# Mixing-stage weight loads issued by ACT behind its casts, and each S5 chunk's preparation on DVE in seven pieces: a layer of S5 and retention heads on one core

## The chip, the cores and the metric

The program runs on 1 core of a Trainium2 chip. The metric is the device time of one execution in microseconds (us); the time of a kernel is the median of its runs. TensorE (PE) multiplies matrices, VectorE (DVE), ScalarE (ACT) and GpSimd (POOL) work elementwise, SyncE (SP) issues DMAs; an engine that issues a DMA does it in the order of its own instructions, and waits there for what the DMA waits for. Each engine runs its instructions in order.

## The reference

One inference step of a layer, with 256 prompt tokens and 8 x 8 sampled tokens, which stand side by side as 320 columns. All arithmetic is fp32.

```python
h = rms_norm(x, norm_mix)
proj = h @ w_in                                  # 2048 x 5120
u, q, k, v, g = split(proj)                      # 5 x 1024 columns
s5_out = s5_mixer(u, ...)                        # 64 groups of 16 channels, 64 complex states each:
                                                 # bu = B u; x_t = lam x_(t-1) + bu_t; y = Re(C x) + d u
                                                 # gelu(y), then y * sigmoid(y @ w_glu + b)
qh, kh = rotary(q), rotary(k) / sqrt(128)        # 8 heads of 128
o, r = retention_chunked(qh, kh, vh, r0)         # (q k^T * decay mask) v + decayed q r0
ret = silu(g) * group_norm(o) * ret_gn_w
x = x + concat(s5_out, ret) @ w_out
gate, up = split(rms_norm(x, norm_ffn) @ w_ffn_in)
x = x + (silu(gate) * up) @ w_ffn_out            # width 5632
return rms_norm(x, norm_final), S5 states, retention states
```

## The kernel before, in words

Every weight matrix is cut into 128 x 128 blocks and read once. `wload` fetches up to eight blocks (128 x 1024 fp32, 512 KB) into a tile `raw`, ACT rounds it to the TensorE format (`hi`, the cast of L131), and DVE takes the rest (`lo = raw - hi`, L133). `gemm` then runs three matmuls for each block, hi by x's hi part, hi by x's lo part, lo by x's hi part (L143 to L145), with all 320 columns. `raw`, `hi` and `lo` have three buffers each, so that load n can start once the tiles of load n-3 are read. One input projection of 128 output columns takes two such loads. The loads are numbered here in the order of the program, from 0; loads 0 to 8 are those of the first four projections, which run together (L976 to L992), and 9 to 96 are the rest of the mixing stage.

The mixing stage (the first 400 us or so) goes through the heads h = 0 to 7: `do_q`, `do_k`, `do_v` (each a projection), for h < 4 also the gate `do_g`, for h < 6 also `do_u`, the S5 input of chunk h + 2; the gates of heads 4 to 7 follow, and then `w_out` for the retention half (`ps_o`). `rot` turns q and k (two copies `sw` on ACT, L748 and L749, three or four products and sums on DVE, among them `k_`). `head_k` transposes k (`pst`), multiplies q by k (`pss`) and scales the transposed k (`kd` on ACT, L765); `head_v` transposes v, ACT copies it (`vT`, L791, and `vs`, L792), and PE sums up the head (`po`, `psr`). DVE takes the statistics of `po` (BN_STATS, L822), POOL makes the scale of them (`gy`, L826 to L833), ACT normalizes (`on`, L839), and PE transposes the result (`pn`).

`s5_chunk(c)` handles an eighth of the S5 channels. It sends u through DRAM into another layout (`up_`, `via`, `kst`), prepares its coefficients on DVE (products `m` of `raw_bc` with the power tables `gpc` and `lpc`, sums `bl` and `cl`, the table `tb` from `e`, and `bst` from `btr` and `gtr`), then PE projects (`pb`) and makes the kernel `pk_`, which ACT copies (`toe`, L684), DVE scans, PE projects back (`py`), ACT and DVE add it up (`ev`), and SP sends it through DRAM again (`back`, `yc`). Then `y1 = d u + yc` on DVE and the GELU of it (ACT L727, L728, L730). In front of all this, the powers of the S5 eigenvalues are computed in many small operations on DVE (`scrt`, `ecs`, `lp`, `ff`, `gp`), copied by ACT into the tables (`lpc` L489, `gpc` L492, `gs` L501), and PE transposes `gs` (`pt`, L107), from which the rows `gtr` come.

PE's and POOL's order is the order in which the program writes them down. The chunks and heads are generators that yield a delay; after each weight block the program's own clock goes up by 0.4, and a generator whose delay has run out writes its next part there, between two blocks. The delays stand in the table `DL`. The order on DVE, ACT and SP is made by a scheduler from priorities (`high_priority`, `issue_after`) and its own costs.

Of the kernel before, what the change touches and what calls it, by code (L numbers as in the profile page):

```python
# [12 lines left out]
F32 = mybir.dt.float32  # L13
# [4 lines left out]
ADD, SUB, MUL = ALU.add, ALU.subtract, ALU.mult  # L18
PSUM = bass.MemoryType.PSUM

P = 128
# [11 lines left out]
CH = 4  # L33
NCP = NP // CH
# [10 lines left out]
def hybrid_kernel(ctx, tc, xT, w_in, w_in4, w_out, w_glu, w_fi, w_fo, vecs, s5p, bc, bt, x0,  # L45
# [3 lines left out]
    pe, act, dve, pool, sp = nc.tensor, nc.scalar, nc.vector, nc.gpsimd, nc.sync  # L49
# [68 lines left out]

    wpool = [wp, (3, 3, 3)]
    last_hi, last_raw, last_lo = [None], [None], [None]  # L120

    def wload(src, nk, offset=3000):

        out = []
        with tc.high_priority(offset=offset):
            for k0 in range(0, nk, 8):
                m = min(8, nk - k0)
                raw, hi, lo = (wpool[0].tile([P, 8, P], d, name=n, tag=n, bufs=wpool[1][i])
                               for i, (n, d) in enumerate((("raw", F32), ("hi", F32R), ("lo", F32R))))
                last_raw[0] = sp.dma_start(raw[:, :m], src[:, k0:k0 + m])  # L130
                cast = act.copy(hi[:, :m], raw[:, :m])  # L131
                last_hi[0] = cast
                last_lo[0] = dve.tensor_tensor(lo[:, :m], raw[:, :m], f(hi[:, :m]), SUB)  # L133
                out += [(hi[:, i], lo[:, i]) for i in range(m)]
        return out
# [41 lines left out]
    def tt(out, a, b, op):  # L177
        dve.tensor_tensor(out, a, b, op)
        return out
# [133 lines left out]
    lpc = s5.tile([P, 8, 2, 8, CH], F32, name="lpc")  # L313
# [248 lines left out]
        pool.tensor_tensor(ta, c8, s1, MUL)  # L562
        pool.tensor_tensor(tabl[:, 1], tabl[:, 1], ta, ADD)

    def s5_table(c):
# [5 lines left out]
        tb = s5.tile([P, 2, 4, NCP], F32, name="tb", tag="tb", bufs=1)  # L571
# [4 lines left out]
        tt(m2[:, 1], c8, s1, MUL)  # L576
        for r, op in enumerate((SUB, ADD)):
            tt(tb[:, r], m1[:, r].rearrange("p j a b -> p j (a b)"), m2[:, r].rearrange("p j a b -> p j (a b)"), op)
        return tb
# [43 lines left out]
    def s5_chunk(c):  # L623
# [16 lines left out]
                        raw[64 * g:64 * g + 64, 1, 4 * q:4 * q + 4], 1.0 - 2.0 * q)  # L640
        with tc.issue_after(rot_t["values"].ins):
            act.copy(d0[:, :, :, 1:], r4[:, js].unsqueeze(1).unsqueeze(3).to_broadcast([P, 2, 4, NCP - 1]))
        for w_, pc in ((0, gpc), (1, lpc)):
            dm = 3 - w_
            shm = [P, 8, CH, 16] if w_ else [P, 8, 16, CH]
            m1, m2 = (s5.tile(shm, F32, name=f"m{q}", tag=f"m{q}", bufs=1) for q in range(2))
            b_ = raw[:, w_].unsqueeze(dm).to_broadcast(shm)
            tt(m1, b_, pc[:, c, 0].unsqueeze(5 - dm).to_broadcast(shm), MUL)
            tt(m2, b_, pc[:, c, 1].unsqueeze(5 - dm).to_broadcast(shm), MUL)
            if w_ == 0:  # L650

                bl = s5.tile([P, 2, 2, 2, 16, CH], F32, name="bl", tag="bl", bufs=1)
                for r, (a, b, op) in enumerate(((m1[:, 0:4], m2[:, 4:8], SUB), (m1[:, 4:8], m2[:, 0:4], ADD))):
                    a, b = (t_.rearrange("p (u q) h s -> p u q (h s)", q=2) for t_ in (a, b))
                    tt(bl[:, r].rearrange("p q u h s -> p u q (h s)"), a, b, op)
                continue
            tt(cl[:, 0], m1[:, 0:4], m2[:, 4:8], SUB)
            tt(cl[:, 1], m1[:, 4:8], m2[:, 0:4], SUB)
        if c:
            tbl = s5_table(c)  # L660
        yield DL["b1"] + (4.0 if c == 0 else 0.0)
        if not c:
            tbl = s5_table(c)
        bst = s5_bst(c).rearrange("p q r s -> p r q s")
        load_bc(c + 2)
        yield DL["b2"]
        pb = ps_b.tile([P, 2, 512], F32, name="pb", tag="pb", bufs=1)
        for i in range(4):
            for u in range(2):
# [273 lines left out]
    def do_g(h):  # L943
        ps = proj(11 + 4 * h)
        sg = mp.tile([P, N], F32, name="sg", tag="sg", bufs=2)
        with tc.high_priority(offset=EVAC):
# [193 lines left out]
    rpool.close()  # L1140
    zhi = glp.tile([P, 8, N], F32R, name="zhi")
    zlo = glp.tile([P, 8, N], F32R, name="zlo")
    for n in range(8):
        ps = gemm("ps_g", w_glu[n], 8, yhi, ylo)
        with tc.issue_after(last_raw[0].ins):
            for g in range(2):
                sp.dma_start(vd[g::2, :, n].rearrange("h t e -> t h e"), vs[64 * g + NS * n:64 * g + NS * n + NS])
        sg = glp.tile([P, N], F32, name="sgl", tag="sgl", bufs=2)
        act.activation(sg, ps, AF.Sigmoid, bias=v("bglu", n))
        stt(sg, u32[:, n], 0.5, sg, MUL, MUL)  # L1150
        act.copy(zhi[:, n], sg)
        tt(zlo[:, n], sg, f(zhi[:, n]), SUB)
# [241 lines left out]
```

## Time and profile before

| | |
|---|---|
| median of 3 runs | 1443.73 us (1443.13 to 1445.22) |
| profiled execution | 1444.08 us, of which the span is 1442.3 us |
| mean granted TensorE clock | 0.994 |
| busy share of the span | PE 98%, DVE 68%, ACT 41%, POOL 8% |
| casts hi (L131) | 416, 969 ns each |
| differences lo (L133) | 416, 1125 ns each |
| weight loads of the mixing stage from `w_in` (L130) | 79 of 512 KB, each holding its issuer 0.33 us |

The span is one execution on the chip; the busy time of an engine holds no waiting. The views used are the waits (which engine waited at which line for which instruction of another, in us in total, times and the longest), the windows (busy time and number of instructions of each engine in a stretch, with the granted clock in the column after POOL, and the share and rate of the DMA engines), the timeline (start, duration, engine, line, operation, tiles, and the idle time before it with what ended it) and the chain of waits that ended last. Pieces overlap a little in the timeline, because an engine starts an instruction before the one before it has drained.

### The profile page before, as it was taken

To read this page: it belongs to the slowest core of one execution; us is meant where nothing else is said; L and a number is where in the kernel's file an instruction comes from. 1 tells how busy PE (TensorE), PEld (TensorE's weight loads), DVE (VectorE), ACT (ScalarE), POOL (GpSimd) and SP (SyncE) were. 2 spreads that over 40 slices of the span, in tenths; PEclk is the share of its full clock that TensorE was granted. 3 is DMA by queue.
4 is the path that set the end of the run, shared out by engine and by line. 5 is a ranking of instruction groups with operands and counts; after the bars stand their busy time and mean duration, and the time that the engine had idled before them with its cause. 6 is when DMAs were issued, how large, how long until landed. Compare 5 with 4: busy or idle time off the path is not lost.

```text
span 1442.3 us, 26157 instructions
## 1 busy us (share of the span) xinstructions
PE 1420.2 (98%) x10364; PEld 1407.3 (98%) x10364; DVE 973.8 (68%) x1917; ACT 591.8 (41%) x937; POOL 111.2 (8%) x177
## 2 busy tenths in 40 slices
PE   9999999999999999999999999999999999999996
PEld 9999999989999999999999999999999999999996
DVE  7988777788766746676777545767644677644554
ACT  7644545454355533333333333333333333333442
POOL 7620010011000000100000000000000000000001
PEclk9999999999999999999999999999999999999998
DMA  8565565555654466666757346666545765444442
GB/s 284 185 196 174 161 192 168 187 151 160 202 164 149 148 217 215 225 227 224 240 201 252 122 154 231 232 219 233 170 147 181 253 229 183 159 127 155 147 150 104
DMA packets 106363, 271.20 MB, mean 188 GB/s; under 512 B 30720, under 2 KB 44288, under 8 KB 106240
## 3 DMA queue, kind: packets, MB, share of 16 engines
q1 hardware_dynamic: 106096, 269.26, 56.2%
q8 instruction: 81, 1.33, 0.4%
q14 instruction: 42, 0.34, 0.1%
q10 hardware_dynamic: 144, 0.26, 0.1%
HBM read 258.44 MB, written 10.65 MB: 187 GB/s over the span
## 4 chain that ended last, share of the span: by engine, by line
PE 92%; DVE 3%; DMA 2%; ACT 2%; issue 0%; SPq 0%; DVEq 0%; ACTq 0%
PE ps_fo L143 7%; PE ps_fu L143 7%; PE ps_fu L144 7%; PE ps_fo L144 7%; PE ps_fo L145 7%; PE ps_fu L145 7%; PE ps_fg L143 7%; PE ps_fg L144 7%; PE ps_fg L145 7%; PE ps_p L143 5%; PE ps_p L145 5%; PE ps_p L144 5%; PE ps_o L143 2%; PE ps_o L144 2%; PE ps_o L145 2%; DVE lo L133 1%
## 5 line engine op out<-in xcount | busy, mean ns | idle before, releaser
L131 ACT CAST hi<-raw 128x1024 fp32r<-128x1024 f32 (+1 forms) x416 | 402.1, 969 | 674.9 <-PE ps_fo L144 187.9
L133 DVE TENSOR_TENSOR lo<-raw,hi 128x1024 fp32r<-128x1024 f32 (+1 forms) x416 | 467.4, 1125 | 299.1 <-ACT hi L131 296.7
L144 PE MATMUL ps_fo<-alo,hi 128*128 128x320 f32 x704 | 217.5, 309 | 0.0
L143 PE MATMUL ps_fg<-hhi,hi 128*128 128x320 f32 x704 | 217.5, 309 | 0.0
L143 PE MATMUL ps_fo<-ahi,hi 128*128 128x320 f32 x704 | 217.5, 309 | 0.0
L145 PE MATMUL ps_fo<-ahi,lo 128*128 128x320 f32 x704 | 217.5, 309 | 0.0
L144 PE MATMUL ps_fu<-hlo,hi 128*128 128x320 f32 x704 | 217.4, 309 | 0.0
L144 PE MATMUL ps_fg<-hlo,hi 128*128 128x320 f32 x704 | 217.4, 309 | 0.0
L145 PE MATMUL ps_fg<-hhi,lo 128*128 128x320 f32 x704 | 217.4, 309 | 0.0
L143 PE MATMUL ps_fu<-hhi,hi 128*128 128x320 f32 x704 | 217.4, 309 | 0.0
L145 PE MATMUL ps_fu<-hhi,lo 128*128 128x320 f32 x704 | 217.4, 309 | 0.0
L143 PE MATMUL ps_p<-xhi,hi 128*128 128x320 f32 x560 | 178.3, 318 | 1.6 <-ACT hi L131 1.6
L145 PE MATMUL ps_p<-xhi,lo 128*128 128x320 f32 x560 | 174.2, 311 | 0.7 <-DVE lo L133 0.7
L144 PE MATMUL ps_p<-xlo,hi 128*128 128x320 f32 x560 | 173.8, 310 | 0.0
L144 PEld LDWEIGHTS ps_fg<-hlo,hi 128*128 128x128 f32 x704 | 132.4, 188 | 0.0
L143 PEld LDWEIGHTS ps_fo<-ahi,hi 128*128 128x128 f32 x704 | 132.4, 188 | 0.0
L143 PEld LDWEIGHTS ps_fu<-hhi,hi 128*128 128x128 f32 x704 | 132.4, 188 | 0.0
L144 PEld LDWEIGHTS ps_fu<-hlo,hi 128*128 128x128 f32 x704 | 132.4, 188 | 0.0
L145 PEld LDWEIGHTS ps_fo<-ahi,lo 128*128 128x128 f32 x704 | 132.4, 188 | 0.0
L143 PEld LDWEIGHTS ps_fg<-hhi,hi 128*128 128x128 f32 x704 | 132.4, 188 | 0.0
L145 PEld LDWEIGHTS ps_fu<-hhi,lo 128*128 128x128 f32 x704 | 132.4, 188 | 0.0
L145 PEld LDWEIGHTS ps_fg<-hhi,lo 128*128 128x128 f32 x704 | 132.3, 188 | 0.0
(459 smaller groups left out, 2065.0 us busy)
## 6 DMA issues: line engine op xcount, KB each, us to landing
raw<-w_fi SPq DMA_DIRECT2D x176, 512.0 KB
raw<-w_in SPq DMA_DIRECT2D x79, 512.0 KB
raw<-w_fo SPq DMA_DIRECT2D x64, 512.0 KB
raw<-w_out SPq DMA_DIRECT2D x32, 512.0 KB
hi<-vd SPq DMA_DIRECT2D x32, 512.0 KB
lo<-vd SPq DMA_DIRECT2D x32, 512.0 KB
raw<-w_fo SPq DMA_DIRECT2D x64, 192.0 KB
rt<-r SPq DMA_DIRECT2D x8, 512.0 KB
```

Of the source, the lines that this page charges most:

```text
L131: cast = act.copy(hi[:, :m], raw[:, :m])
L133: last_lo[0] = dve.tensor_tensor(lo[:, :m], raw[:, :m], f(hi[:, :m]), SUB)
L143: pe.matmul(ps, hi, xhi[:, k], start=k == 0, stop=False)
L144: pe.matmul(ps, hi, xlo[:, k], start=False, stop=False)
L145: pe.matmul(ps, lo, xhi[:, k], start=False, stop=k == nk - 1)
```

## The change

`wload` no longer issues all raw loads on SP. While `on_act` is true, that is for loads 9 to 96, load n is issued by ACT, directly behind cast n-2. From the gated projection (`w_glu`) on, all loads stand on SP as before. So 88 loads move from SP's queue into ACT's.

In `s5_chunk` the preparation on DVE, which was written in two lumps around the yields `b1` and `b2`, is now written in seven pieces, each behind the last `lo` on DVE, with eight equal yields of the same sum (20.8, or 24.8 for chunk 0). The table function is cut in two for this. The delay `rows` goes from 11.0 to 12.5.

```diff
@@ wload
-                last_raw[0] = sp.dma_start(raw[:, :m], src[:, k0:k0 + m])
+                if on_act[0]:
+                    with tc.issue_after(casts[-2].ins) if len(casts) > 1 else ExitStack():
+                        act.dma_start(raw[:, :m], src[:, k0:k0 + m])
+                else:
+                    last_raw[0] = sp.dma_start(raw[:, :m], src[:, k0:k0 + m])
                 cast = act.copy(hi[:, :m], raw[:, :m])
+                casts.append(cast)
@@ s5_chunk
-        for w_, pc in ((0, gpc), (1, lpc)):
...
-        if c:
-            tbl = s5_table(c)
-        yield DL["b1"] + (4.0 if c == 0 else 0.0)
-        if not c:
-            tbl = s5_table(c)
-        bst = s5_bst(c).rearrange("p q r s -> p r q s")
-        load_bc(c + 2)
-        yield DL["b2"]
+        def paced(*fs):
+            with tc.issue_after(last_lo[0].ins):
+                return [g() for g in fs][-1]
+
+        step = (DL["b1"] + DL["b2"] + (4.0 if c == 0 else 0.0)) / 8
+        paced(lambda: powers(0, 0))
+        yield step
+        bl = paced(lambda: powers(0, 1), bl_sums)
+        yield step
+        paced(lambda: powers(1, 0))
+        yield step
+        paced(lambda: powers(1, 1), cl_sums)
+        yield step
+        em = paced(lambda: s5_table1(c))
+        yield step
+        tbl = paced(lambda: s5_table2(em))
+        yield step
+        bst = paced(lambda: s5_bst(c)).rearrange("p q r s -> p r q s")
+        yield step
+        load_bc(c + 2)
+        yield step
@@
-    DL = dict(b1=14.2, b2=6.6, scan=17.8, y=10.0, rows=11.0, k=8.5, v=6.1,
+    DL = dict(b1=14.2, b2=6.6, scan=17.8, y=10.0, rows=12.5, k=8.5, v=6.1,
@@ before the loop over w_glu
+    on_act[0] = False
```

(`powers(w_, q)` is one of the four products `m`, `bl_sums` and `cl_sums` the sums made of two of them.) A yield lets the program go on until its clock has passed the delay, and the clock moves in steps of a block, so PE's order moves with the yields: `pb` and `pk_` of a chunk stand 9 to 24 matmuls later among the matmuls of the projections, `py` 6 to 24 later, the two transposes `pt` 12 later. The scheduler, which has other dependences now, puts DVE and ACT into another order in many places. The changed file's lines are some 6 to 30 higher.

DVE around the turned k of head 0 (`k__737`; `lo` are the differences of the weights, `qg`, `qsp`, `ksp` parts of the turned q and k, `sg` a gate, `scrt`, `ecs`, `lp` the powers). Before:

```order
L178 TENSOR_TENSOR k__737<-ps_p,csr 128x320
L178 TENSOR_TENSOR sw<-sw,csr 128x320
L178 TENSOR_TENSOR ecs<-scrt 128x2x32
L178 TENSOR_TENSOR k__737<-k__737,sw 128x256
L178 TENSOR_TENSOR ksp<-k__737,sw 128x64
L178 TENSOR_TENSOR sg<-ps_p,rbc 128x320
L178 TENSOR_TENSOR lp<-rr,ecs 128x32 x2
L178 TENSOR_TENSOR scrt<-prm 128x32 x2
L178 TENSOR_TENSOR qg_111<-qsp,gqt 128x4x8
L133 TENSOR_TENSOR lo<-raw,hi 128x1024
```

And now:

```order
L184 TENSOR_TENSOR qsp<-q__727,sw 128x64
L184 TENSOR_TENSOR scrt<-prm 128x32
L184 TENSOR_TENSOR qg_111<-qsp,gqt 128x4x8 x2
L184 TENSOR_TENSOR scrt<-scrt 128x32
L442 RECIPROCAL scrt<-scrt 128x32
L184 TENSOR_TENSOR k__737<-ps_p,csr 128x320
L184 TENSOR_TENSOR sw<-sw,csr 128x320
L184 TENSOR_TENSOR sg<-ps_p,rbc 128x320
L139 TENSOR_TENSOR lo<-raw,hi 128x1024
L184 TENSOR_TENSOR k__737<-k__737,sw 128x256
L184 TENSOR_TENSOR ksp<-k__737,sw 128x64
L184 TENSOR_TENSOR sm<-pss,mk 128x256
```

The last sum of k, on which PE's transposes `pst` wait, has moved behind a gate, a difference lo and all the small operations that came after it, and stands directly ahead of `sm`, which needs PE's product of q and k.

ACT around the copies `gs` of the S5 powers, whose last four PE's transposes `pt` wait for. The casts here are those of loads 17, 18 and 19. Before:

```order
L131 CAST hi<-raw 128x1024
L492 COPY gpc<-gp 128x8x8 x6
L501 COPY gs<-gp 128x2x16 x6
L131 CAST hi<-raw 128x1024
L839 ACTIVATE on<-po,gy 128x128 x2
L508 COPY gt<-pt 128x256
L131 CAST hi<-raw 128x1024
```

And now:

```order
L136 CAST hi<-raw 128x1024
L133 DMA raw<-w_in 128x1024
L498 COPY gpc<-gp 128x8x8 x6
L136 CAST hi<-raw 128x1024
L133 DMA raw<-w_in 128x1024
L869 ACTIVATE on<-po,gy 128x128 x2
L507 COPY gs<-gp 128x2x16 x2
L136 CAST hi<-raw 128x1024
L133 DMA raw<-w_in 128x1024
L778 COPY sw<-ps_p 64x320
L779 COPY sw<-ps_p 64x320
L507 COPY gs<-gp 128x2x16 x4
```

Of the six copies four have moved behind two more casts, three loads and two copies `sw`. The last cast is that of load 19, and load 19 is the first DMA of this piece.

ACT around the head whose `po` stood at 319 us, head 7 (`v_r` is a cast of a finished head, `y` the GELU of an S5 chunk). Before:

```order
L727 ACTIVATE y_4333<-y_4332 128x320
L628 COPY up__4602<-u_118 128x320
L728 ACTIVATE y_4333<-y_4333,ones 128x320
L791 ACTIVATE vT<-pst_4361,rtok 128x128 x3
L1094 CAST v_r<-retp 128x320
L730 ACTIVATE y_4333<-y_4333 128x320
L131 CAST hi<-raw 128x1024
L792 COPY vs<-vT 64x128
```

And now:

```order
L638 COPY up__4609<-u_118 128x320
L821 ACTIVATE vT<-pst_4353,rtok 128x128 x3
L1124 CAST v_r<-retp 128x320
L136 CAST hi<-raw 128x1024
L133 DMA raw<-w_in 128x1024
L822 COPY vs<-vT 64x128
L757 ACTIVATE y_4363<-y_4362 128x320
```

The copies `vT` and `vs` of the head, for which PE's `po` waits, stood behind the first and second step of the GELU and now stand ahead of it; `vs` has a cast and a load ahead of it.

Two more places are told in words. In head 3 DVE had the statistics of `po` (L822) behind the two sums `tb` and three of the products `e` of a chunk's table, and now has these behind the statistics. And in five of the eight chunks `y1`, which waits for `yc`, has moved up on DVE ahead of a q, a k or a difference lo; in chunk 4 (`y1` at 282 us before) it now stands ahead of the lo of load 67 and of the turned k of head 6, and on ACT the GELU's first step, which waits for `y1`, stands ahead of cast 68 and its load, of `up_`, of cast 69 and its load and of `v_`, and `toe` behind all of these.

More of the change, by code (lines that the diff above doesn't have):

```diff
@@ L120, in hybrid_kernel @@
     last_hi, last_raw, last_lo = [None], [None], [None]
+    casts, on_act = [], [True]
     def wload(src, nk, offset=3000):
@@ L563, in s5_turns, with s5_table1 @@
         pool.tensor_tensor(tabl[:, 1], tabl[:, 1], ta, ADD)
-    def s5_table(c):
+    def s5_table1(c):
         js = slice(4 * c, 4 * c + 4)
@@ L570, in s5_table @@
         c8, s8 = (e18[:, 1, r, js].unsqueeze(3).to_broadcast(sht) for r in range(2))
-        tb = s5.tile([P, 2, 4, NCP], F32, name="tb", tag="tb", bufs=1)
         m1, m2 = (s5.tile([P, 2, 4, 8, 8], F32, name=f"e{q}", tag=f"m{q}", bufs=1) for q in range(2))
@@ L576, in s5_table, with s5_table2 @@
         tt(m2[:, 1], c8, s1, MUL)
+        return m1, m2
+    def s5_table2(ms):
+        m1, m2 = ms
+        tb = s5.tile([P, 2, 4, NCP], F32, name="tb", tag="tb", bufs=1)
         for r, op in enumerate((SUB, ADD)):
@@ L642, in s5_chunk, with powers @@
             act.copy(d0[:, :, :, 1:], r4[:, js].unsqueeze(1).unsqueeze(3).to_broadcast([P, 2, 4, NCP - 1]))
-        for w_, pc in ((0, gpc), (1, lpc)):
+        prods = {}
+        def powers(w_, q):
             dm = 3 - w_
+            pc = (gpc, lpc)[w_]
             shm = [P, 8, CH, 16] if w_ else [P, 8, 16, CH]
[L646 to L656, printed above, removed]
+            prods[q] = s5.tile(shm, F32, name=f"m{q}", tag=f"m{q}", bufs=1)
+            tt(prods[q], raw[:, w_].unsqueeze(dm).to_broadcast(shm),
+               pc[:, c, q].unsqueeze(5 - dm).to_broadcast(shm), MUL)
@@ new lines, in bl_sums, with cl_sums @@
+        def bl_sums():
+            m1, m2 = prods[0], prods[1]
+            bl = s5.tile([P, 2, 2, 2, 16, CH], F32, name="bl", tag="bl", bufs=1)
+            for r, (a, b, op) in enumerate(((m1[:, 0:4], m2[:, 4:8], SUB), (m1[:, 4:8], m2[:, 0:4], ADD))):
+                a, b = (t_.rearrange("p (u q) h s -> p u q (h s)", q=2) for t_ in (a, b))
+                tt(bl[:, r].rearrange("p q u h s -> p u q (h s)"), a, b, op)
+            return bl
+        def cl_sums():
+            m1, m2 = prods[0], prods[1]
```

## The prediction

> **What bounds the kernel now.** I read the busy times first, then PE's waits, then the windows around them, then each wait's cause in the timelines.
>
> ```profile
> PE 1420.2 (98%) x10364; PEld 1407.3 (98%) x10364; DVE 973.8 (68%) x1917; ACT 591.8 (41%) x937; POOL 111.2 (8%) x177
> ```
>
> PE does almost nothing but work. Neither SP's issue time nor the 41% of ACT decides anything as such; a change can only win back PE's gaps or make new ones. PE's waits between 60 and 360 us:
>
> ```profile
> PE ps_p L143 <- ACT hi L131: 1.6, 1, 1.6
> PE po L102 <- ACT vs L792: 1.6, 1, 1.6
> PE po L102 <- ACT vT L791: 1.3, 1, 1.3
> PE pss L102 <- ACT toe L684: 1.2, 1, 1.2
> PE pt L107 <- ACT gs L501: 1.1, 1, 1.1
> PE ps_o L162 <- DVE r L178: 0.9, 1, 0.9
> PE ps_p L145 <- DVE lo L133: 0.7, 1, 0.7
> ```
>
> Together 8.4 us. Two of the places cost more than their idle time, because the granted clock (the number after POOL's) drops behind them:
>
> ```profile
> 190.00:195.00 5.00, 2.97 (x11) 2.66 (x12) 4.17 (x5) 3.17 (x6) 0.00 (x0) 0.75 0.53 190
> 195.00:200.00 5.00, 5.00 (x33) 5.00 (x33) 2.07 (x5) 2.10 (x4) 0.00 (x0) 0.90 0.84 263
> ...
> 280.00:285.00 5.00, 3.79 (x26) 3.55 (x26) 2.74 (x5) 2.10 (x6) 0.00 (x0) 1.00 0.34 116
> ...
> 320.00:325.00 5.00, 2.89 (x32) 2.40 (x36) 4.08 (x9) 3.54 (x10) 0.00 (x0) 0.72 0.71 190
> 325.00:330.00 5.00, 5.00 (x36) 4.60 (x29) 4.90 (x16) 0.78 (x5) 2.65 (x3) 0.59 0.53 150
> ```
>
> Busy time by the missing share of the clock: 2.97 x 0.25 + 5 x 0.10 = 1.2 us behind the waits of 1.6 and 0.7; 2.89 x 0.28 + 5 x 0.41 = 2.9 us behind those of 1.3 and 1.6. The single wait of 1.2 us at 283 left the clock at 1.00. So I price two close waits of 2.3 us or more at 1.2 to 2.9 us beside themselves, one of about 1.2 at nothing.
>
> [...]
>
> **The change part by part.** Every sum is made against the profiled execution, 1444.08 us (span 1442.3 and 1.8 around it); the median is 0.35 lower, and I take this off at the end.
>
> *Head 3's wait at 189 us.* ACT's normalization waited for POOL's scale, and the cast that PE wanted stood behind it:
>
> ```profile
> 183.24 0.75 DVE L178 TENSOR_TENSOR tb<-e,e 128x256 f32<-128x256 f32 x2
> 183.91 0.49 DVE L822 BATCH_NORM_STATS2 st<-po 128x6 f32<-128x128 f32 x2
> ```
>
> ```profile
> 188.63 1.16 ACT L839 ACTIVATE on<-po,gy 128x128 f32<-128x128 f32 x3 [6.79 <-POOL gy L833]
> ```
>
> The two `tb` that began at 183.24 took 0.67 us until the statistics began, 0.33 each; the three `e` have the same shape and are taken at the same price. These five now stand behind the statistics, 1.7 us together. Everything behind them comes 1.7 us earlier, which is the wait of 1.6 for the cast and takes 0.3 of the 0.7 for the lo. With the clock: -(1.6 + 0.3 + 1.2) = **-3.2** (bounds -2.0 and -3.5).
>
> *Head 7's waits at 319 us.* `vT` and `vs` stood behind a GELU that waited for `yc`:
>
> ```profile
> 318.65 0.47 ACT L727 ACTIVATE y<-y 128x320 f32<-128x320 f32 x1 [4.42 <-DMA raw<-w_in]
> ...
> 322.70 0.29 ACT L792 COPY vs<-vT 64x128 f32<-64x128 f32 x1
> ```
>
> They are ahead of it now. What is left is a cast and a load between `vT` and `vs`, and `po` now ahead of `pb` and `pk_`, so PE asks earlier; I leave 1.3 of the 2.9 us, too little to lower the clock. -(1.6 + 2.9) = **-4.4** (bounds -3.0, if the clock still falls a little, and -5.8, all of it).
>
> *Head 0's k at 52 us: a new wait.* Before, the last sum of k was done 0.3 us before PE's transposes:
>
> ```profile
> 51.49 0.41 DVE L178 TENSOR_TENSOR k__737<-k__737,sw 128x256 f32<-128x256 f32 x1
> ...
> 52.00 0.48 DVE L178 TENSOR_TENSOR sg<-ps_p,rbc 128x320 f32<-128x320 f32 x1
> ...
> 55.46 0.36 DVE L178 TENSOR_TENSOR sm<-pss,mk 128x256 f32<-128x256 f32 x1
> ```
>
> ```profile
> 52.19 0.38 PE L107 MATMUL pst<-ident,k__737 128*128 128x128 f32 x2
> ```
>
> All that DVE did from 52.00 to 55.46 (a gate, `lp`, `scrt`, `qg`, a lo, the reciprocal) now comes ahead of that sum: 3.5 us, less the 0.3 of slack. DVE is full here (the rows join without gaps), so it can't be early. PE waits about 3.2 us (bounds 2.4 and 4.5, the last if load 9, which goes out behind cast 7, is also late).
>
> *The copies `gs` at 67 us: a wait that grows.* ACT's rows of before give the price of each piece, and the chain of waits two weight loads from issue to landing:
>
> ```profile
> 64.92 1.05 ACT L131 CAST hi<-raw 128x1024 fp32r<-128x1024 f32 x1
> 65.86 1.04 ACT L492 COPY gpc<-gp 128x64 f32<-128x64 f32 x6
> 66.73 0.84 ACT L501 COPY gs<-gp 128x32 f32<-128x32 f32 x6
> 67.45 1.07 ACT L131 CAST hi<-raw 128x1024 fp32r<-128x1024 f32 x1
> ...
> 70.45 0.42 ACT L748 COPY sw<-ps_p 64x320 f32<-64x320 f32 x1
> ```
>
> ```profile
> 0.72 3.51 DMA raw<-w_in
> ...
> 21.98 5.67 DMA raw<-w_in
> ```
>
> ```profile
> 269.50 0.33 SPq L130 DMA_DIRECT2D raw<-w_in  x1
> ```
>
> DVE is some 1.4 us late behind `sm`, so cast 17 runs 66.4 to 67.4. Load 19 leaves behind it and lands 3.5 to 5.7 us later; I take 4.1, the nearer to the end without other transfers. Cast 19 to 72.6, a load of 0.33, two `sw` of 0.42, four `gs` of 0.12 each: 74.3, and 0.4 for the transposes. Before, PE was through them at 67.7; 12 matmuls of 0.147 us that now come first make 69.5. PE is 5.2 us behind here, head 0's wait included. The clock falls behind that wait, but PE waits for ACT again at `pt`, which swallows the loss; only what falls behind `pt` is new, 0.7. **+5.9** for both (bounds 4.3 and 7.5).
>
> *Chunk 4's `y1` at 282 us.* It waits for `yc` and now stands ahead of lo 67 and k on DVE, and on ACT the GELU ahead of two casts and `toe`:
>
> ```profile
> 276.01 6.02 DMA yc<-back
> ```
>
> ```profile
> 313.05 2.16 SPq L721 DMA_DIRECT2D yc<-back  x3
> ```
>
> ```profile
> 317.81 0.76 DVE L182 SCALAR_TENSOR_TENSOR y<-u,vec,yc 128x320 f32<-128x320 f32 x1 [3.76 <-DMA yc<-back]
> ```
>
> In chunk 4 the last `yc` took 6 us from issue to landing; in the next chunk `y1` could begin 2.6 us after the last `yc` was issued (313.05 + 2.16). If it is so quick here, `toe` is done as late as before: 0. If it lands at 282 again, `y1` (0.7), y, cast 68 (1.05), a load, y, `up_`, cast 69 (1.05), a load, `v_`, `toe` follow: 288.0 where `pss` began at 284.8, +3.2, and the clock falls, 1.2 to 2.9 more. I take a landing in the middle, 280.3: **+1.3** (bounds -1.2 and +6.1).
>
> *The rest.* The same step up of `y1` ahead of k in chunk 0: +0.3 (0 to 1). At 350 the casts `r` stand behind a cast and a load more: +0.4 (bounds -0.9, the wait gone, and +0.8). The 88 issues are 88 x 0.33 = 29 us of ACT, 7% of the 400 us of the stage; they cost where a load stands between a wait and its release, and are counted there. That load n leaves only behind cast n-2 leaves 5 us for cast, issue and landing (1.05 + 0.33 + 3.5, at worst 7.1) against two tiles of PE's work, 48 matmuls of 0.147 = 7.1 us: covered, with no room at the worst landing. Without this cover each late load would be a wait of its own. SP without the loads brings nothing to PE: none of the waits above ends on a DMA.
>
> Sum: 1444.08 - 3.2 - 4.4 + 5.9 + 1.3 + 0.3 + 0.4 = 1444.4; less 0.35: **1444.0 us**, no change within 0.2% (2.9 us), which is about what a measurement of this kernel tells from none.
>
> **The rivals.** (a) Faster: `yc` early (no wait added at 283, and the 1.2 there gone: -2.5 against the sum) and nothing lost behind `pt`, with load 19 in 3.5 us (-1.3): 1444.0 - 3.8 = 1440.2. For it: SP has no weight loads between `back` and `yc` any more. Against: `yc` needs 6.0 us in one chunk and 3.0 in another, and shares the DMA engines with the same loads.
>
> (b) Slower, one mechanism: DVE and ACT stand still for `yc` at 276 to 282 us, with lo 67, k, two casts and `toe` behind. It decides from a landing after 280 us on; at 282 it costs 3.2 + 1.2 to 2.9 in place of 1.3: 1444.0 + 3.1 to 4.8 = 1447 to 1449. For it: the row of 6.02 us. Against: SP issues `yc` earlier.
>
> (c) The new order at 319 doesn't do what it says: the load between `vT` and `vs` waits for a lo or an earlier DMA, and the wait and the clock stay: 1444.0 + 4.4 = 1448.4. For it: a load on ACT's queue holds everything behind it. Against: there the weights are well ahead.
>
> **How the numbers follow.** Forecast (within 0.2%) 0.38; (a) and other ways to the fast side 0.29; (b) 0.2, (c) and others 0.13. So faster 0.29, same 0.38, slower 0.33. The bounds of all terms on one side give 1437 and 1453; the range that leaves out about 2 in 10 is 1438.5 to 1450.5; the forecast's own is 1441.0 to 1446.8.
>
> **What would show it.** PE's waits would list `pst` on DVE's k at 52 us with about 3 us, and `pt` on `gs` with 1 to 3 us; the waits for the cast hi at 189 and for `vs` at 319 would be gone or below 1.2, the clock 1.00 at 190 to 200 and 320 to 330, and below 1.00 somewhere in 55 to 80. `toe` at 283 shows which of (a) and (b) it is. I am wrong if `pst` doesn't wait, or if a wait on a cast or lo appears that ends on a weight load.

## The result and the profile after

The changed kernel takes 1448.58 us (median; 1445.82 to 1453.09) against 1443.97 us (1442.31 to 1446.70) of the kernel before on the same chip: a ratio of 1.0033 [1.0024, 1.0043], slower by 4.6 us. The prediction was 1444.0 with a range of 1438.5 to 1450.5; the time lies in the range, but outside the forecast's own 1441.0 to 1446.8 and on the side that had a chance of 0.33. The profiled execution of the changed kernel takes 1447.48 us with a span of 1445.5 (before: 1444.08 and 1442.3), so the trace shows 3.2 of the 4.6 us.

Busy times on the page of the changed kernel:

```profile
PE 1420.4 (98%) x10364; PEld 1407.0 (97%) x10364; DVE 972.4 (67%) x1917; ACT 592.8 (41%) x937; POOL 100.2 (7%) x177
```

PE, DVE and ACT are as busy as before (POOL is at work 11 us less): the work is the same, and the loss is again in PE's gaps. PE's waits between 20 and 420 us (engine and line that waited, for what, us in total, times, the longest):

```profile
PE pst L107 <- DVE k__737 L184: 4.4, 1, 4.4
PE ps_p L151 <- DVE lo L139: 3.9, 5, 1.5
PE ps_o L168 <- DVE r L184: 3.1, 1, 3.1
PE pt L107 <- ACT gs L507: 0.8, 1, 0.8
PE pss L102 <- ACT toe L714: 0.5, 1, 0.5
```

The waits for the cast at 189 and for `vT` and `vs` at 319 are gone. In their place stand the new wait for head 0's k, five for a lo, and one for `r` that has grown from 0.9 to 3.1. Windows of the changed kernel (busy us of PE, PEld, DVE, ACT and POOL, granted clock, DMA share and GB/s):

```profile
55.00:60.00 5.00, 2.68 (x13) 2.56 (x14) 4.05 (x11) 2.38 (x7) 4.69 (x10) 0.80 0.37 117
...
190.00:195.00 5.00, 5.00 (x73) 4.91 (x64) 2.82 (x12) 0.00 (x0) 2.15 (x7) 1.00 0.74 247
...
320.00:325.00 5.00, 5.00 (x60) 4.88 (x62) 1.63 (x3) 3.15 (x7) 0.00 (x0) 1.00 0.75 213
...
355.00:360.00 5.00, 4.82 (x23) 4.82 (x24) 3.15 (x9) 0.46 (x1) 0.00 (x0) 0.67 0.88 222
```

The clock is full at 190 and 320, where it was 0.75 and 0.72, and below full behind the waits for k and for `r`.

To see where the time goes I took from the traces, for each weight load, the start of its first matmul on PE in both traces, and the difference (after less before) from load to load. What it gains or loses between two loads belongs to the work between them:

| place | load to load | difference goes from, to | change | predicted |
|---|---|---|---|---|
| start: k at 52, `pt` at 67 | 13 to 19 | 0.6 to 6.0 | +5.4 | +5.9 |
| 150 to 170: waits for lo | 35 to 43 | 6.0 to 8.7 | +2.8 | none |
| head 3 at 189 | 45 to 47 | 8.7 to 5.1 | -3.7 | -3.2 |
| chunk 4 at 283 | 57 to 75 | 5.4 to 5.0 | -0.4 | +1.3 |
| head 7 at 319 | 75 to 77 | 5.0 to -0.9 | -5.9 | -4.4 |
| 338: a wait for a lo | 77 to 79 | -0.9 to 0.7 | +1.6 | none |
| `r` at 355 | 79 to 83 | 0.7 to 3.8 | +3.1 | +0.4 |

Pieces of under 0.5 us are left out; the last matmul of the program is 3.8 us later.

**k at 52 to 57 us.** DVE's timeline, and PE's:

```profile
50.30 1.54 DVE L139 TENSOR_TENSOR lo<-raw,hi 128x1024 fp32r<-128x1024 f32 x1
...
53.51 0.43 DVE L184 TENSOR_TENSOR k__737<-ps_p,csr 128x320 f32<-128x320 f32 x1
53.85 0.86 DVE L184 TENSOR_TENSOR sw<-sw,csr 128x320 f32<-128x320 f32 x1
54.64 0.48 DVE L184 TENSOR_TENSOR sg<-ps_p,rbc 128x320 f32<-128x320 f32 x1
55.04 1.34 DVE L139 TENSOR_TENSOR lo<-raw,hi 128x1024 fp32r<-128x1024 f32 x1
56.31 0.86 DVE L184 TENSOR_TENSOR k__737<-k__737,sw 128x256 f32<-128x256 f32 x1
```

```profile
57.32 0.41 PE L107 MATMUL pst<-ident,k__737 128*128 128x128 f32 x2 [4.42 <-DVE k__737 L184]
```

k's sum stands behind `sg` and a lo, as the order said, and starts at 56.31 instead of 51.49. But several rows are slow: `sw` and the sum take 0.86 us each where they took 0.48 and 0.41 before.

**A lo at 150 to 160 us.** ACT, then DVE:

```profile
150.90 0.46 ACT L869 ACTIVATE on<-po,gy 128x128 f32<-128x128 f32 x1 [4.61 <-POOL gy L863]
...
151.60 1.04 ACT L136 CAST hi<-raw 128x1024 fp32r<-128x1024 f32 x1
```

```profile
152.68 1.23 DVE L139 TENSOR_TENSOR lo<-raw,hi 128x1024 fp32r<-128x1024 f32 x1 [4.69 <-ACT hi L136]
...
158.15 2.35 DVE L139 TENSOR_TENSOR lo<-raw,hi 128x1024 fp32r<-128x1024 f32 x2
```

This cast is that of load 36. It stands behind head 2's normalization `on`, which waits 4.6 us for POOL's scale; in the kernel before it ran at 140.06 us, ahead of the `on` at 146.54. So DVE, with its preparation tied behind the lo of that cast, stands still for 4.7 us and then has 4.3 us of preparation ahead of the next lo, for which PE waits 1.5 us. At 338 the cause is similar: head 7's `on` waits 3.5 us for POOL. Cast 78 stands behind it in both kernels, but now the copies `ends` do too; DVE waits 2.6 us for them, and the lo stands behind the rows that wait with it.

**r at 355 us.** DVE, then PE:

```profile
353.64 0.75 DVE L184 TENSOR_TENSOR bt__4879<-btr,gtr 128x256 f32<-128x256 f32 x2
354.31 0.41 DVE L184 TENSOR_TENSOR btr<-btr,gtr 128x256 f32<-128x256 f32 x1
354.65 1.69 DVE L184 TENSOR_TENSOR r<-retp,r 128x320 fp32r<-128x320 f32 x4
```

```profile
355.18 0.64 PE L168 MATMUL ps_o<-r,hi 128*128 128x320 f32 x1 [3.06 <-DVE r L184]
```

The preparation of the last chunk stands ahead of the differences `r`. The first `r` starts 2.8 us later than before (354.65 against 351.83), and PE comes to this place 0.7 us later.

### The profile page after: what moved, and what is told of

Same layout as the page of the kernel before. It is cut to its first block, busy times and chain, and to the rows that moved or that the text cites. A ratio compares the mean times of both kernels' runs of the same rounds, so it can differ in the third digit from the quotient of the medians.

```text
span 1445.5 us, 26143 instructions
## 1 busy us (share of the span) xinstructions
PE 1420.4 (98%) x10364; PEld 1407.0 (97%) x10364; DVE 972.4 (67%) x1917; ACT 592.8 (41%) x937; POOL 100.2 (7%) x177
## 4 chain that ended last, share of the span: by engine, by line
PE 86%; DVE 6%; DMA 4%; issue 1%; ACT 1%; SPq 1%; POOL 0%; ACTq 0%; DVEq 0%; POOLq 0%
PE ps_fo L150 7%; PE ps_fu L150 7%; PE ps_fu L151 7%; PE ps_fo L149 7%; PE ps_fo L151 7%; PE ps_fu L149 7%; PE ps_fg L150 7%; PE ps_fg L151 7%; PE ps_fg L149 7%; PE ps_p L149 3%; PE ps_p L151 3%; PE ps_p L150 3%; PE ps_o L149 2%; PE ps_o L151 2%; PE ps_o L150 2%; DMA raw<-w_in 2%
```

## The experiments

Each kernel was timed beside the kernel before; the ratio is to that, and kernels of different groups are compared by their ratios. All of them compute the whole output.

| | us | ratio [95%] | span |
|---|---|---|---|
| the change | 1448.58 | 1.0033 [1.0024, 1.0043] | 1445.5 |
| loads on ACT alone | 1451.44 | 1.0054 [1.0041, 1.0066] | 1448.4 |
| pieces alone, rows 11 | 1439.52 | 0.9972 [0.9961, 0.9982] | 1439.6 |
| change without the loads on ACT | 1439.29 | 0.9965 [0.9953, 0.9977] | 1439.7 |
| change, loads 9 to 15 on SP | 1442.03 | 0.9988 [0.9979, 0.9997] | 1440.7 |
| change, pieces not tied behind the lo | 1450.08 | 1.0047 [1.0035, 1.0060] | 1447.6 |
| pieces alone, head 0's k late | 1443.96 | 0.9989 [0.9980, 0.9998] | 1440.4 |
| change, head 2's `on` later | 1444.32 | 1.0000 [0.9992, 1.0009] | 1442.3 |
| pieces alone, last table later | 1439.93 | 0.9968 [0.9956, 0.9980] | 1438.5 |
| loads 9 to 15 on SP, head 2's `on` later | 1439.03 | 0.9953 [0.9941, 0.9965] | 1435.7 |
| no loads on ACT, head 2's `on` later | 1437.77 | 0.9943 [0.9930, 0.9956] | 1436.6 |
| change, POOL's turns later | 1449.48 | 1.0024 [1.0015, 1.0034] | 1448.1 |
| no loads on ACT, `on` and table later | 1436.27 | 0.9934 [0.9922, 0.9946] | 1434.3 |

**1. Each part alone.** The loads on ACT with the preparation as it was:

```diff
-        paced(lambda: powers(0, 0))
-        yield step
...
+        if c:
+            tbl = s5_table(c)
+        yield DL["b1"] + (4.0 if c == 0 else 0.0)
...
-    DL = dict(b1=14.2, b2=6.6, scan=17.8, y=10.0, rows=12.5, k=8.5, v=6.1,
+    DL = dict(b1=14.2, b2=6.6, scan=17.8, y=10.0, rows=11.0, k=8.5, v=6.1,
```

> Only the first part of the change: loads 9 to 96 on ACT behind the casts; the S5 preparation in its two lumps and rows = 11.0 as before. Theory (A), the loads on ACT make the new order at the start and the pieces make the new waits on lo and r: the start loses 6 us as in the changed kernel (k of head 0 stands in the same late place on DVE), the waits for lo at 154 to 160 and 338 us and the 3 us on r at 355 are not there, head 3's wait (3.7) is gone because the statistics of po stand ahead of cl and e here too, head 7's wait stays in part (vs still stands behind the GELU): 1444.0 + 6.0 - 3.7 - 1.5 = about 1445, and PE's waits for lo and r under 1.5 us together. Theory (B), the loads on ACT come too late and starve the casts, and the pieces are innocent: the waits for lo (3.9) and r (3.1) are there as well, about 1450, and the waits of the casts on raw loads are long.

The pieces, with the loads left on SP:

```diff
-    casts, on_act = [], [True]
+    casts, on_act = [], [False]
...
-    DL = dict(b1=14.2, b2=6.6, scan=17.8, y=10.0, rows=12.5, k=8.5, v=6.1,
+    DL = dict(b1=14.2, b2=6.6, scan=17.8, y=10.0, rows=11.0, k=8.5, v=6.1,
```

> Only the second part: the preparation in seven paced pieces, all loads on SP, rows = 11.0. (A): the start is that of before (k of head 0 early, gs in one piece: loss 0); head 3's wait (-3.7) and head 7's (-5.8) go, since vT and vs stand ahead of the GELU and the statistics ahead of the table here too; the waits that pieces make stay (lo at 154 to 172: 2.8, lo at 338: 1.6, r at 355: 3.1): 1444.0 - 9.5 + 7.5 = 1442. (B): these waits belong to the loads on ACT and go too: 1444.0 - 9.5 = 1434.5.

And the change with nothing undone but the loads (rows at 12.5):

```diff
-    casts, on_act = [], [True]
+    casts, on_act = [], [False]
```

> The whole change with the loads left on SP: pieces and the delay rows of 12.5. It differs from the whole change in the loads alone. If the delay of the rows does nothing of its own, the time is that of the pieces alone, 1439.5, and the loads' share is +9; if the later rows cost or gain, it shows as more than 1.5 us of difference from 1439.5.

The two halves have opposite signs. The pieces gain 4 to 5 us, 0.9972 and 0.9965, and the later rows do nothing that can be told. The loads on ACT lose 7.8 us alone and 9.8 us on top of the pieces (1.0033 less 0.9965, of 1444). In the second pair the spans differ by 5.8 us only: the profiled execution of the change lies low among its times (1447.48) and that of the other high (1441.47, of 1438.47 to 1441.82). So the traces show 5.8 of the 9.8 us. The first three of PE's waits with the loads on ACT alone, and all of them with the pieces alone:

```profile
PE pst L107 <- DVE k__737 L184: 4.3, 1, 4.3
PE ps_p L149 <- ACT hi L136: 2.4, 3, 1.1
PE ps_p L151 <- DVE lo L139: 2.1, 3, 0.7
```

```profile
PE ps_o L168 <- DVE r L184: 2.5, 1, 2.5
PE pss L102 <- ACT toe L714: 2.4, 1, 2.4
PE ps_p L151 <- DVE lo L139: 1.3, 3, 0.7
PE ps_o L167 <- ACT r L1124: 1.1, 1, 1.1
```

Neither expectation gives the time of its kernel. The loads alone take 1451.44 where theory A gave 1445, because waits for casts, for lo and for `r` (1.8 and 1.4 us) are there without the pieces too. The largest new loss, 3.9 us at 237 us, is again two casts behind an `on`, which waits 7.5 us for POOL there. The pieces alone take 1439.52, between A's 1442 and B's 1434.5.

The late k is the loads' doing: it is in the first kernel and not in the second. The two good terms, heads 3 and 7, come with either half: by the same table as above the pieces alone win 4.0 and 5.9 us there, and the loads alone 2.5 and 5.4. Put together the two halves win them once (3.7 and 5.9). The wait for `r` is in both.

The wait for `toe`, 2.4 us with the pieces alone, is 0.5 in the whole change, and this is a gain of the loads. In chunk 4 `y1` can begin 2.5 us after the last `yc` was issued (282.11 to 284.62), in the change without the loads 4.9 us (273.94 to 278.88). In the seven kernels here that have the loads from 16 on on ACT this takes 2.5 to 3.2 us and PE waits at most 0.5 us for `toe`; in the seven that have them on SP it takes 4.7 to 5.6 us and PE waits 1.0 to 3.0. How late PE is doesn't decide it: in the first group PE lies anywhere from 9.7 us behind the kernel before to 5.4 ahead of it at load 66. It is what rival (a) named, an early `yc`; whether it is SP's freer queue that does it is not shown. The part of the loads that the trace shows is so 7.2 us lost at the start (the difference at load 33 is 6.0 with them and -1.2 without), of which 3.4 come back at `toe`, and 2 us more at the waits for lo and `r`.

**2. Which loads.** The whole change, with the first seven of the loads left on SP:

```diff
+FIRST_ACT = 16
...
-                if on_act[0]:
+                if on_act[0] and len(casts) >= FIRST_ACT:
```

> The whole change, but ACT issues only from load 16 on; loads 9 to 15 stand on SP as before. k of head 0 and the six gs are then in the old places. (A): the 6 us of the start go, all else stays: 1448.6 - 6 = 1442.6, no wait of pst for k above 0.5 us. A rival for the start, that seven pieces fill DVE there and k is late for want of DVE time: the wait of 4.4 us stays and the time is 1448.

1442.03, a ratio of 0.9988: theory A. With loads 9 to 15 on SP, k waits for nothing, and at load 33 PE is 1.3 us ahead of the kernel before instead of 6.0 behind. 6.5 of the 9.8 us hang on seven of 88 loads. The other 3.3 us are the difference between this kernel and the change without any load on ACT (0.9988 and 0.9965, and the intervals don't meet; 1.0 us by the spans). PE's waits for lo are longer here, 5.5 us in all against 1.9 there.

**3. Is it the tie behind the lo?** The whole change, the seven pieces in their places, without the tie:

```diff
         def paced(*fs):
-            with tc.issue_after(last_lo[0].ins):
-                return [g() for g in fs][-1]
+            return [g() for g in fs][-1]
```

> The whole change, but the seven pieces are not tied behind the last lo (the eight equal yields stay). If the waits for lo at 154 to 172 us come from DVE standing idle for a cast with preparation tied behind the lo of that cast, they go: -2.8, and part of the 3.1 at r: 1448.6 - 3 to 5 = 1444 to 1446. If they come from the yields or from the loads, the waits and the time stay: 1448. The start keeps its 6 us either way.

1450.08: no better, if anything worse. DVE's idle time ahead of the lo at 153 halves, 2.35 us instead of 4.69, but PE's waits for lo are still 3.1 us, four of them. My explanation of the loss by the pacing falls with that.

**4. The late k: order or late loads?** The pieces alone, with one thing added: head 0's sum of k is written later and tied behind the RECIPROCAL, so that it has its place of the whole change. Every other row of the three engines keeps its order but for `sg`, `qg` and that lo, which close up:

```diff
-        dve.reciprocal(rden, den)
+        rot_t["recip"] = dve.reciprocal(rden, den)
...
-        tt(a[:, 0:NP], a[:, 0:NP], sw[:, 0:NP], ADD)
+        if name == "k_" and "late" not in HS[0]:
+            HS[0]["late"] = sw
+        else:
+            tt(a[:, 0:NP], a[:, 0:NP], sw[:, 0:NP], ADD)
...
+        if h == 0:
+            with tc.high_priority(offset=EVAC), tc.issue_after(rot_t["recip"].ins):
+                tt(k_[:, 0:NP], k_[:, 0:NP], HS[0]["late"][:, 0:NP], ADD)
         pst = misc("pst")
```

> The pieces alone (loads on SP), as before, with one thing added: head 0's last sum of k on DVE is tied behind the RECIPROCAL and so stands behind a gate, the powers and a lo, directly ahead of sm, which is its place in the whole change; every other row on DVE, ACT and PE stays. Theory A (the loss at the start of the whole change comes from DVE's order, and not from loads that land late or from ACT): PE's pst waits for k about 3 us at 52, the matmuls behind it fall back by 4 to 6 us against the pieces alone, and the time goes from 1439.5 to 1443.5 to 1445.5. Theory B (the order of that sum matters little; the loads on ACT themselves are late at the start): pst waits less than 1.5 us and the time stays below 1441.5.

PE's wait and the window behind it:

```profile
55.07 0.41 PE L107 MATMUL pst<-ident,k__737 128*128 128x128 f32 x2 [2.17 <-DVE k__737 L184]
```

```profile
55.00:60.00 5.00, 4.87 (x34) 4.66 (x35) 3.83 (x14) 3.26 (x11) 4.69 (x8) 1.00 0.58 167
```

By the ratios the late k costs 2.5 us (0.9989 against 0.9972 of the pieces alone), or 3.5 against the kernel with the later rows (0.9965), which was timed in the same group. The trace agrees with the smaller price: a wait of 2.2 us, not 3, no loss of clock, and matmuls 1.8 us later than with the pieces alone. So the order does cost, as theory A has it, but less than its 4 to 6 us, though 1443.96 stands inside the times that it gave. The place of the sum is worth half of the wait of 4.4. The other half is in what stands ahead of it: in the whole change k's first product also starts 3.4 us later (53.51 against 50.12 without the loads), behind the powers; and in the slow rows, the next experiment.

**5. Why DVE's rows are slow there.** In the whole change POOL works on the tables `e`, `ta` and `tabl` from 48.5 to 60 us, beside the late k. The same kernel, with these operations written behind the scores of head 0; no row of DVE or PE moves, and on ACT a few load issues and, from 250 us on, two others do:

```diff
-        s5_turns(ec, es)
+        rot_t["turns"] = (ec, es)
...
         if h == 0:
+            s5_turns(*rot_t["turns"])
             with tc.issue_after(last.ins):
```

> The whole change, with POOL's turns (the operations on e, ta and tabl, which ran from 48.5 to 60 us beside the late k) written behind the scores of head 0, so that POOL stands still until k is done; no row of DVE, ACT or PE moves. Theory A (DVE's instructions took up to twice their time there because POOL worked beside them: lo 1.54 and 1.34 against 1.22, sw and k 0.86 against 0.48 and 0.42): they take their usual times, k's sum begins some 1.5 us earlier, PE's wait for it falls from 4.4 to about 2.9, and the time by 1.5 to 2.5, to 1446 to 1447. Theory B (they are slow for another reason): the wait stays 4.4 and the time 1448.6.

The window from 48 to 57 us, first of the change, then of the kernel with POOL still:

```profile
48.00:57.00 9.00, 4.90 (x34) 4.64 (x32) 8.96 (x22) 5.18 (x8) 8.13 (x13) 1.00 0.50 153
```

```profile
48.00:57.00 9.00, 6.44 (x44) 6.15 (x43) 7.70 (x26) 5.92 (x11) 0.70 (x5) 1.00 0.52 166
```

With POOL at work DVE needed 8.96 us for 22 rows; with POOL still, 7.70 us for 26. The rows have their usual times again, in DVE's timeline of that kernel:

```profile
53.73 0.48 DVE L184 TENSOR_TENSOR sw<-sw,csr 128x320 f32<-128x320 f32 x1
...
54.53 1.22 DVE L139 TENSOR_TENSOR lo<-raw,hi 128x1024 fp32r<-128x1024 f32 x1
55.66 0.42 DVE L184 TENSOR_TENSOR k__712<-k__712,sw 128x256 f32<-128x256 f32 x1
```

From the same row (`u<-pb`) on, k's sum starts 7.8 us later (47.83 to 55.66) instead of 9.3 (47.05 to 56.31): the 1.5 us that theory A gave, near enough. Theory A is right on the mechanism; its gain in time doesn't show. By the ratios the kernel is 1.3 us quicker than the change (1.0024 against 1.0033, and the intervals overlap), by the spans 2.6 us slower. The wait for k falls to 2.6, and two others grow:

```profile
PE pst L107 <- ACT kd L795: 2.8, 1, 2.8
PE pst L107 <- DVE ksp L184: 2.6, 1, 2.6
PE pt L107 <- ACT gs L507: 2.4, 1, 2.4
```

POOL's work, done later (56.74 to 67.28 us), stands beside DVE's next rows, and those are slow (two `ff` at 59.64 take 0.66 us, two `scrt` at 60.22 1.29, where either pair took 0.28 in the change). POOL's own scale for head 0, which stands behind it, comes late: its first `gy` starts at 67.98 us instead of 65.17. What was won ahead of k is lost by 75 us, at the wait for `gs`. The wait of 2.8 us for `kd` stands at 186 us, behind a load issue for which ACT waited; the runs don't show whether POOL's work has to do with it.

**6. The cast behind the normalization.** In the whole change, head 2's `on` written as head 0's is, behind the second next cast:

```diff
-        if h:
+        if h not in (0, 2):
             normed()
...
-        if not h:
+        if h in (0, 2):
```

> The whole change, with ACT's normalization of head 2 tied behind the second next cast (as the program does it for head 0), so that cast 36 no longer stands behind an instruction that waits 4.6 us for POOL. Theory A (the 2.8 us lost at 150 to 170 come from the cast that stands behind that wait, since DVE's lo and the preparation tied behind it stand still with it): DVE's idle time of 4.7 us at 148 to 153 shrinks below 1.5, PE's waits for lo at 154 to 160 (0.3 and 1.5) go, and the time falls from 1448.6 by 2 to 3 us, to about 1446. Theory B (DVE is too full there, or the raw load lands late anyway): the waits for lo stay above 1 us there, 1448 to 1449.

1444.32, ratio 1.0000: theory A, with a larger gain than expected, 4.8 us by the ratios, 3.2 by the spans. ACT's rows, then DVE's:

```profile
150.52 1.05 ACT L136 CAST hi<-raw 128x1024 fp32r<-128x1024 f32 x1
...
155.05 0.81 ACT L869 ACTIVATE on<-po,gy 128x128 f32<-128x128 f32 x2
```

```profile
153.42 1.21 DVE L139 TENSOR_TENSOR lo<-raw,hi 128x1024 fp32r<-128x1024 f32 x1
```

The second lo, which came at 158.15, comes at 153.42; PE waits for no lo there, and behind head 3 the difference to the kernel before is 2.1 us instead of 5.1. The control is the same edit without the loads on ACT:

> The kernel without the loads on ACT (pieces, rows 12.5), with the normalization of head 2 tied behind the second next cast. It is the control for the same edit in the whole change. If a cast that stands behind the normalization costs time only where the loads on ACT have made the casts late (theory A), this changes little: 1438 to 1439.5 (its one wait for a lo of 1.5 us at 150 may go). If the edit is a gain in itself (theory B), it gains 4 us here too: 1435.

1437.77 against 1439.29: by the ratios 3.2 us gained here too, between the two theories and nearer to B's 4. So the loads on ACT don't make this stall. It is there without them, in the change without the loads:

```profile
143.26 0.81 ACT L869 ACTIVATE on<-po,gy 128x128 f32<-128x128 f32 x2 [4.60 <-POOL gy L863]
```

and DVE's lo behind it waits 4.68 us, at 145.04. With the loads on ACT alone DVE waits 2.35 us there, in the kernel before not at all. Either part of the change brings cast 36 behind the `on`, and the pieces, which tie DVE's preparation to the lo, make DVE's wait twice as long.

**7. Both places undone.** Loads 9 to 15 on SP, and head 2's `on` later:

> The whole change with two places undone: loads 9 to 15 stay on SP (the first 60 us), and the normalization of head 2 is tied behind the second next cast. Theory A (what the loads on ACT cost is these two places and nothing else): the two gains add, 6.5 us from the first and 4.3 from the second on 1448.6, so the time is that of the kernel without the loads on ACT, 1439 to 1440, or a little below. Theory B (the loads cost something at many places, each instruction of ACT behind an issue that waits for a lo): 1441 to 1442.5, since the second gain is partly the same delay as the first.

1439.03, theory A: the two gains add up. Against the kernel with the same `on` and no loads on ACT at all (1437.77) it is 1.3 us slower by the medians and 0.9 quicker by the spans, which is no difference that these runs can tell. So the 81 loads from load 16 on cost nothing measurable where head 2's `on` stands later, and 3.3 us by the ratios where it stands in its place (experiment 2). In the trace they aren't without effect here either: PE loses 4.0 us at 338 us with them and 1.6 without, and wins 0.7 back at `toe` and 2.8 at `r`.

**8. The wait for r.** The pieces alone, the last chunk's table written behind `toe`, ahead of the scan that reads it:

```diff
-        em = paced(lambda: s5_table1(c))
+        if c < 7:
+            em = paced(lambda: s5_table1(c))
...
+        if c == 7:
+            tbl = s5_table2(s5_table1(c))
         with tc.high_priority(offset=2 * EVAC if c == 7 else 0):
             s5_scan(c, pb, xp, d0, tbl)
```

> The pieces alone (loads on SP), with the table of the last chunk (four e, two tb) written behind the copy toe, ahead of the scan that reads it, and not among the paced pieces. Theory A (the wait for r at 346 to 348 is DVE's: six instructions of the table stand ahead of r): r comes 1.4 us earlier, PE's wait for r falls from 2.5 to about 1.1, and the time from 1439.5 to about 1438.1. Theory B (r waits for ACT's casts, which stand behind ev and a cast): the waits for r stay 3.6 in all, 1439.5.

```profile
PE ps_o L168 <- DVE r L184: 1.4, 1, 1.4
PE ps_o L167 <- ACT r L1128: 1.1, 1, 1.1
```

The wait is DVE's by 1.1 us (2.5 to 1.4), as theory A has it; the 1.1 for ACT's cast stays. The span is 1.1 us shorter too (1438.5 against 1439.6), but the time, 1439.93, shows none of it: 0.9968 against 0.9972. 1.1 us is 0.08%, under what these runs tell.

**9. All that helped, in one kernel:** loads on SP, the pieces, head 2's `on` later, the last table later.

> The loads on SP, the pieces, the normalization of head 2 behind the second next cast, and the last chunk's table behind the copy toe: all that helped, in one kernel. If the wait for the lo at 150 (1.5) and that for r (1.2 of 2.5) go and nothing takes their place, 1437 to 1438; if each is met by a later wait, as the table's gain alone was in its time (1439.9), 1439 to 1440.

1436.27, ratio 0.9934 [0.9922, 0.9946]: 9.5 us faster than the kernel before and 14 faster than the change (by the ratios), and under the 1437 that was the lowest expected. Its waits for lo, r and `toe` are 1.5, 1.4 and 1.2, and 1.0 us.

## Where the prediction held and where it failed

The forecast was no change at 1444.0; the kernel is slower by 4.6 us. That the time still lies in the range is luck: in the trace two items cost 7.1 us more than the sum gave them (the waits for lo 4.4, `r` 2.7), and the other terms came out 4.5 us lower. Step by step:

- *Head 3, -3.2:* right, -3.7. The wait for the cast is gone, the clock 1.00. (The sum added 1.6 and 0.3 us of wait for rows that come 1.7 earlier; 1.7 was all that this step could give.)
- *Head 7, -4.4:* the mechanism right, the size too small: -5.9, just past my bound of -5.8. I left 1.3 us of wait there for a cast and a load between `vT` and `vs`; nothing was left. Rival (c) is out.
- *Head 0's k and the copies `gs`, +5.9 together:* right in the sum (+5.4) and wrong in its shares. I gave k a wait of 3.2 and `pt` 1 to 3. k had 4.4, at my upper bound but for other reasons than the late load I named there, with the clock down to 0.80, and `pt` 0.8. So the sum is right by luck. The place alone, which I priced at 3.2, is worth 2.2; DVE's rows beside POOL add 1.4, and the rest may be the powers ahead of k. I read "DVE is full here" and took the durations from the rows of before, though a row that moves may come to stand beside another engine's work and take twice as long, as this sum did beside POOL (0.86 us against 0.41).
- *Chunk 4's `y1`, +1.3:* -0.4, inside the bounds. `y1` waits for `yc` indeed, until 284.62, 2.5 us after the last `yc` was issued (278.11 and 4.00 us for the four), as quickly as the row of 2.6 allowed. DVE and ACT do stand still for `yc`, as rival (b) says, but PE waits only 0.4 us for the lo and 0.5 for `toe`. The kernel is slower, but not by rival (b). This part of rival (a) came true: `yc` is early with the loads on ACT, as experiment 1 shows, and the wait for `toe` goes from 1.2 to 0.5.
- *Chunk 0's `y1`, +0.3:* nothing; the difference stays at 6.0 from load 19 to load 35.
- *r at 350, +0.4:* wrong, +3.1, far past my bound of +0.8. I read ACT's casts alone, and what holds `r` is DVE, with the last chunk's preparation ahead of it: `r` is 2.8 us later than before and PE 0.7. With the last table written later, in the pieces alone (experiment 8), the wait for DVE's `r` falls by 1.1 us.
- *What no term held, +4.4:* the waits for lo at 150 to 170 (+2.8) and at 338 (+1.6). I wrote that the loads are covered and asked for waits that end on a weight load. None of them does. These end on a lo that stands late because an `on` which waits for POOL holds ACT: the cast of load 36 at 150, the copy `ends` at 338. Moving head 2's `on` takes the first away, which shows the cause there; the one at 338 is read from the trace alone. ACT's waits of the kernel before, between 40 and 400 us, have it as their largest, and I read it at 188 only, where the change took it away, and didn't ask where else the new order puts a cast or a copy behind an `on`:

```profile
ACT on L839 <- POOL gy L833: 42.1, 7, 7.3
```

- *That the issues cost 0.33 us each where they stand between a wait and its release:* right for the 81 loads from 16 on once head 2's `on` is out of the way (up to 3.3 us before that), and missing the point for the first seven. Those cost 6.5 us with the order in which DVE does the powers and head 0's q and k. I had this order in the term of k, but as part of "the change", not as the price of the loads. The price of the loads, 7.8 to 9.8 us, and the gain of the pieces, 4 to 5, stand in the prediction unseparated, so I couldn't see that one half of the change would do better alone.

What stays open: why the ratios put 9.8 us on the loads where the two profiled executions differ by 5.8; and the share of the powers ahead of k, which was not tried by itself (4.4 less 2.2 for the place of the sum and 1.4 for POOL leaves some 0.8).

## What to carry to other kernels

A DMA issue on a compute engine's queue cost little here as an instruction (0.33 us), and its price was in the order that the scheduler made around it: look for the one chain that has no slack (here k of the first head, on a DVE that was busy for 8.96 of 9 us) before counting issue times. An instruction that waits for a slow chain of another engine should never stand ahead of a cast or a lo on which others are queued; the largest wait of a lightly used engine, here ACT's for POOL, is the place to look, and moving one such instruction back was worth 3 to 5 us. A change in two parts is to be priced in two sums, and a gain that either part brings (here heads 3 and 7) counts once. A wait that has shrunk or grown should be traced to the row that ends it before it is put down to PE's being late or early: `toe` and `r` both turned out to have moved themselves.

## What the runs showed of the hardware

Some of DVE's instructions took longer here while POOL worked beside them, and others didn't. In the change, from 50 to 57 us: lo (two inputs in SBUF) 1.54 and 1.34 against 1.22, `sw` 0.86 against 0.48, k's sum 0.86 against 0.42, while `sg` and k's first product, which read PSUM and one tile in SBUF, took 0.48 and 0.43 as ever. A row of POOL's took longer as well; it stands here as in the change, and with POOL's work put later:

```profile
50.84 1.29 POOL L558 TENSOR_TENSOR ta<-e,ecs 128x128 f32<-128x128 f32 x1
```

```profile
58.64 0.47 POOL L558 TENSOR_TENSOR ta<-e,ecs 128x128 f32<-128x128 f32 x1
```

The first was under way while the lo of 1.54 ran (50.30 to 51.84), and ended 0.3 us behind it. Two inputs in SBUF alone don't make a row slow: in the kernel with POOL's work put later, a lo at 62.30 took 1.22 us with a row of POOL's beside it, which took 1.62 (62.41). What else decides, the runs don't show.

The granted clock fell here behind single waits shorter than I had a row for, but the length of the wait doesn't settle it. Behind 1.46 us (159 us, the change) and 2.17 us (k written late, window above) it stayed at 1.00; behind 2.39 us (the wait for `toe`, in the pieces alone) it fell to 0.67:

```profile
280.00:285.00 5.00, 3.15 (x11) 2.97 (x12) 4.23 (x12) 3.44 (x12) 0.00 (x0) 0.67 0.74 231
```

This looks like a limit between 2.2 and 2.4 us, and two other traces speak against it. With loads 9 to 15 on SP and head 2's `on` later, the clock fell behind 1.72 us (and 0.16 shortly before); with loads 9 to 15 on SP alone, it was full from 355 to 360 us, behind a wait of 3.08 us that ended at 351.74 (the mean clock of that execution, 0.997, is the highest of those profiled):

```profile
327.93 0.41 PE L152 MATMUL ps_p<-xhi,lo 128*128 128x320 f32 x1 [1.72 <-DVE lo L140]
```

```profile
330.00:335.00 5.00, 5.00 (x31) 5.00 (x30) 4.93 (x9) 2.71 (x5) 0.00 (x0) 0.83 0.51 182
```

```profile
351.74 0.42 PE L169 MATMUL ps_o<-r,hi 128*128 128x320 f32 x1 [3.08 <-DVE r L185]
```

```profile
355.00:360.00 5.00, 5.00 (x36) 5.00 (x35) 3.54 (x5) 2.10 (x2) 0.00 (x0) 1.00 0.96 283
```

So the clock fell behind 1.72 and 2.39 us, and was full behind 1.46 and 2.17 us and, from 3.3 us after its end, behind 3.08 us; what beside the length of the wait decides it, no run here tests.
